# Second layer's attention: the queries' sums of squares in four units between products, and the key row behind the rotation of the queries

## The chip, the cores and the metric

The kernel runs on one core of one Trainium2 chip. The core has a matrix engine (TensorE, PE in the profile; PEld is its loading of weights), a vector engine (DVE), a scalar engine (ACT), GpSimd (POOL) and a queue that issues transfers (SP). Each engine works through its own list of instructions and waits on semaphores of the others. The metric is the device time of one execution in microseconds (us), the median of three runs; lower is better. For this kernel a difference of 0.3%, some 4.9 us, is about what a measurement can tell from none.

## The reference, cut to what matters

The program is two transformer blocks in float32 on 512 tokens of width 1024. The change lies in the second layer of the first block, an attention of eight heads:

```python
def mla_layer(x, positions, k_sh, v_sh, norm_g, w_in, q_lat_g, w_q_up, q_gain, w_out, mk, mv, mq_gain):
    ...
    q = (rmsnorm(q_lat, q_lat_g) @ w_q_up).reshape(bsz, s, B_HEADS, QK_HEAD)
    q = rmsnorm(q, q_gain)
    q = jnp.concatenate([q[..., :QK_NOPE], rope(q[..., QK_NOPE:], positions)], axis=-1)
    attn = chunk_causal_attention(q, k_sh, v_sh).reshape(bsz, s, B_WIDTH)
    y_b = attn * jax.nn.silu(z)
    ...
```

A query or key of a head has 192 numbers: 128 without a position and 64 that are rotated by the position. Both are normalised by the root of their mean square over all 192. The kernel does not scale queries and keys before the product: it multiplies the scores of a query by its factor, and the scores of a key by the key's. So it needs, for each head and token, the sum of squares of the query and of the key.

## The kernel before, in words

Every float32 product is made of three products of a coarse and a fine half (`mm3`, lines 519 to 522): high by high, high by low, low by high. So weights are split on the way: ACT writes the high half (`whi`, line 285 or 292), DVE the low one (`wlo`, line 286 or 293). Activations are split in the same way in `split` (lines 534 to 540).

The program is a list of units that is worked through in order; there is no scheduler behind it, and each engine's instructions stand in the order in which the units issue them. A unit that multiplies by weights leaves a second part (its post, for instance a split of the product) that is issued when the next unit begins; between units, pieces of the next weights' split are issued on ACT and DVE.

The eight heads go in four groups of two (g = 0 to 3). `prep(g)` makes what a group needs, as a list of units:

- `kn(h)`: the keys of one head (`kn`, and their squares); `kss(h)`: the keys' sums of squares by products with a column of ones (`ssk`). The second one starts the inverse root (`rsqrt`: two DVE instructions, then ten small POOL instructions that end in `rsx`, line 562).
- `qr`: the 64 rotated numbers of both heads' queries in one product, their squares, and the split for the rotation (`rph`, `rpl`); `qn(h)`: the other 128 of each head.
- `krow`: the key factors as rows. PE transposes them (`rkT`, line 1425), ACT copies them out (`rr`, 1427), POOL stores them to DRAM (`rd`, 1429) and then, when that has landed, loads them back broadcast over 128 partitions for each head (`rkb`, 1432).
- `qrot`: the rotation (`rope_rotate`): two products on PE (`rot`), three DVE instructions (`ra`, `rb`, `ra`; lines 1265 to 1267), then a split of the result: `qrh` on ACT, `qrl` on DVE.
- `qss`: the queries' sums of squares (`ssq`): for each of four blocks of 128 tokens one product with a two-column matrix and two with a column of ones, each of which the profile shows as two instructions, 24 in all; then the inverse root.
- `vu(0)`, `vu(1)`: the values.

`attend(g)` has eight scores, one for each head and block of queries. A score is: products on PE (`sc`), a DVE pass that multiplies by `rkb` and takes the maximum (line 1496), `nb`, the exponential on ACT, then on DVE the reciprocal and `e` times it (1505, 1506), then transposes of `e` on PE (`pt`, 1512), and their split into `PTh` and `PTl`. After four scores the product with the values follows (`po`). In the list, a score, the normalisation of the one before it and the transposes of the one two before it make a step; the units of the next group's `prep` and of the output product of the group before (`outproj`, `op`: six products of 512 columns to a unit) are dealt out between the eleven steps (`weave`).

The first group's `prep` has no attention beside it: it stands alone behind the gates' products.

Of the kernel before, what the change touches and what calls it, by code (L numbers as in the profile page):

```python
# [26 lines left out]
def block_kernel(ctx: ExitStack, tc: tile.TileContext, A: dict, out: bass.AP, stop=None):  # L27
# [23 lines left out]
    def bank(shape, name):  # L51
        return psum.tile(shape, F32, tag="b", name=name)

    def T(name="t", dt=F32):
        return tmp_p.tile([128, 512], dt, tag="T", name=name)

    def tiny(n, name):
        return tiny_p.tile([128, n], F32, tag=name, name=name)

    def pair(p, shape, tag, bufs=None):  # L60
        kw = {} if bufs is None else {"bufs": bufs}
        return (p.tile(shape, F32R, tag=tag + "h", name=tag + "h", **kw),
                p.tile(shape, F32R, tag=tag + "l", name=tag + "l", **kw))
# [244 lines left out]
    def U(fn, *keys, early=False, quiet=False):  # L308


        return (fn, keys, early, quiet)

    def add(*units):
        for u in units:
            if isinstance(u, list):
                add(*u)
            else:
                prog.append(u)
# [223 lines left out]
    def newton(v, n, eng=None, tiles=None):  # L542

        y, x, t = tiles or (tiny(n, f"{n_}{n}") for n_ in ("rsy", "rsx", "rst"))
        eng = eng or pool
        dve.tensor_scalar(out=y.bitcast(I32), in0=v.bitcast(I32), scalar1=-0.5, scalar2=float(0x5F19E900), op0=ALU.mult, op1=ALU.add)  # L546
        eng.tensor_tensor(out=x, in0=y, in1=y, op=ALU.mult)  # L547
        if n == 1:
            eng.tensor_scalar(out=x, in0=x, scalar1=v, scalar2=-0.7468889355659485, op0=ALU.mult, op1=ALU.add)
            src = x  # L550
            for c, by in ((-0.87124263, x), (0.77787455, x), (-0.77461322, x), (1.15710291, y)):
                eng.tensor_scalar(out=t, in0=src, scalar1=c, scalar2=by, op0=ALU.add, op1=ALU.mult)
                src = t
            return t
        eng.tensor_tensor(out=x, in0=x, in1=v, op=ALU.mult)

        for o, a in ((t, -0.33874717354774475), (x, -1.5906518697738647)):
            eng.tensor_scalar(out=o, in0=x, scalar1=a, scalar2=None, op0=ALU.add)
            eng.tensor_tensor(out=o, in0=o, in1=o, op=ALU.mult)
        for o, b, by in ((t, 0.8454821109771729, y), (x, 0.4313766062259674, t)):  # L560
            eng.tensor_scalar(out=o, in0=o, scalar1=b, scalar2=None, op0=ALU.add)
            eng.tensor_tensor(out=o, in0=o, in1=by, op=ALU.mult)
        return x

    def rsqrt(ssq, n, inv_d, post=1.0):
        v = tiny(n, "nv" if n == 1 else f"rsv{n}")
        dve.tensor_scalar(out=v, in0=ssq, scalar1=inv_d / post ** 2, scalar2=EPS / post ** 2, op0=ALU.mult, op1=ALU.add)
        return newton(v, n)
# [817 lines left out]
    H = {}  # L1386

    def prep(g):
# [11 lines left out]
        def kn(h):  # L1400
            def post(ps):
                sq = H["ksq", g, h] = T("sq")
                act.activation(out=sq, in_=ps, func=AF.Square)
                k = H["kn", g, h] = pair(bh.p, [128, 512], "kn", bufs=3)
                split(k[0], k[1], ps, scale=g_nope)

            return fmu(kkey, 128 * h, post, src="cT", nk=2)

        def kss(h):
            def fn():  # L1410
                if h == 0:
                    H["kss", g] = bank([128, 2, 4], "ssk")
                sq = H.pop(("ksq", g, h))
                for tb in range(4):
                    pe.matmul(out=H["kss", g][:, h, tb:tb + 1], lhsT=sq[:, tb * 128:tb * 128 + 128], rhs=ones, start=True, stop=True)
                if h == 1:
                    sk = tiny(8, "fac").rearrange("p (a b) -> p a b", a=2)
                    dve.tensor_tensor(out=sk, in0=H.pop(("kss", g)), in1=S["ssp"].unsqueeze(1).to_broadcast([128, 2, 4]), op=ALU.add)
                    H["rk", g] = rsqrt(sk.rearrange("p a b -> p (a b)"), 8, 1.0 / 192)

            return U(fn)
# [33 lines left out]
        def qn(h):  # L1455
            def post(ps):
                sq = T("sq")
                H["qsq", g].append(sq)
                act.activation(out=sq, in_=ps, func=AF.Square)
                q = H["qn", g, h] = pair(bh.p, [128, 512], "qn", bufs=3)  # L1460
                split(q[0], q[1], ps)

            return fmu(qkey, 128 * h, post, src="qlT", nk=3)

        def qss():
            sp = bank([128, 4, 2], "ssq")
            sqs = H.pop(("qsq", g))
            for tb in range(4):
                t = slice(tb * 128, tb * 128 + 128)
                pe.matmul(out=sp[:, tb, :], lhsT=sqs[0][:, t], rhs=blk1, start=True, stop=False)  # L1470
                for h in range(2):
                    pe.matmul(out=sp[:, tb, h:h + 1], lhsT=sqs[1 + h][:, t], rhs=ones, start=False, stop=h == 1)
            H["cq", g] = rsqrt(sp.rearrange("p a b -> p (a b)"), 8, 1.0 / 192, post=192 ** -0.5)

        qr = fmu(qkey, 256, qr_post, src="qlT", nk=3)
        return ([kn(0), kss(0), kn(1), kss(1), qr, qn(0), qn(1), U(krow), U(qrot), U(qss)],
                [vu(0), vu(1)])

    def attend(g):
# [56 lines left out]
    def pt_view(i, j):  # L1536
# [3 lines left out]
        return S["PT"][i][:, at:at + 384 * (j + 1)].rearrange("p (k c) -> p k c", c=384)[:, :, c:c + 128]  # L1540

    preps = [prep(g) for g in range(4)]
    add(U(open_bh))
    add([preps[0][0][i] for i in (0, 2, 1, 4, 3, 5, 6, 7, 8, 9)], preps[0][1])
    for g in range(4):
        m = outproj(f"oB{g - 1}", b_w_out, 2 * (g - 1), 2, slots=((g - 1) % 2,)) if g else []
        if g < 3:
            p = preps[g + 1][0]
            if g:
                m = m[0:2] + p[0:1] + m[2:4] + p[1:2] + m[4:6] + p[2:3] + m[6:8] + p[3:]  # L1550
            else:
                a0 = attend(0)
                add(weave(a0[0:6], p[0:1] + ob[4:5] + p[1:2] + ob[5:7] + p[2:3] + ob[7:8] + p[3:4]), weave(a0[6:], p[4:]), preps[1][1])
                continue
        if g < 3:
            add(weave(attend(g), m, lead=0), preps[g + 1][1])
        else:
            st3 = attend(g)
            ckl, ckn, _ = mem_norm(mem2_in, A["g_mem_2"], None, raw=lambda i: [S["bz"][:, 2 * i + h, :] for h in range(2)],
                                   gp=lambda: [S["bz"][:, 4 + h, :] for h in range(2)])  # L1560
            oB2 = m
            add(ckl, weave(st3[0:5], m[0:4]))
# [674 lines left out]
```

## Time and profile before

| | |
|---|---|
| median of 3 runs | 1630.41 us (1627.05 to 1632.39) |
| the profiled execution | 1630.76 us, its span 1629.0 us |
| PE busy | 1559.9 us (96%) |
| DVE, ACT, POOL busy | 1071.3, 743.3, 312.5 us |
| mean granted clock of PE | 0.987 |

The span is what the trace covers, so the execution has 1.8 us around it. A granted clock of 1.00 is 2.4 GHz, one of 0.50 is 1.2 GHz. The attention of the second layer lies between 645 and 842 us. A profile's row gives the start, the duration, the engine, the line, the instruction with its output and inputs, its shape, and in brackets how long the engine sat idle ahead of it and which instruction ended that. Rows of neighbours with one line are merged, and matmuls overlap, so that a start is a better mark than a duration.

### The profile page before, as it was taken

Reading aid. Unit: us, or ns where it says so; the run is one execution under the profiler, and the core shown is the slowest. Engines: PE = TensorE matmul, PEld = TensorE weight load, DVE = VectorE, ACT = ScalarE, POOL = GpSimd, SP = SyncE. Lnnn points to the kernel's source line nnn. Section 1 sums busy time; section 2 is a strip of 40 time slices with the busy share of each in tenths; the row PEclk is TensorE's granted clock in tenths of the full one; section 3 lists DMA queues with packets and bytes.
Section 4 is the critical chain, followed back from the end, with each engine's and each line's share of the span. In section 5 each row is a group of like instructions: output and inputs, shape, how many; then the busy total and the mean of one; then the engine's idle time right before and its main releaser. Section 6 shows DMA issues by size and latency. Waiting matters only on the chain. (4 is left out here: it accounts for less than half of the span.)

```text
span 1629.0 us, 24253 instructions
## 1 busy us (share of the span) xinstructions
PE 1559.9 (96%) x9385; PEld 1354.0 (83%) x9385; DVE 1071.3 (66%) x1980; ACT 743.3 (46%) x1538; POOL 312.5 (19%) x570
## 2 busy tenths in 40 slices
PE   6999999999999999999989999989999999999996
PEld 6889898988788888778869877868878889898986
DVE  6567646565685563667777555577456579686968
ACT  5344424333465544445544333455333463636353
POOL 4100000000030100211211000012100265555552
PEclk9999999999999999999999999999999999999998
DMA  8422223221332221212324331233312224141411
GB/s 265 140 78 70 87 78 90 67 92 65 129 112 83 91 78 35 92 35 67 124 72 148 116 118 52 73 109 117 99 70 73 76 85 156 52 156 52 142 53 52
DMA packets 134795, 152.75 MB, mean 94 GB/s; under 512 B 7616, under 2 KB 120024, under 8 KB 134680
## 3 DMA queue, kind: packets, MB, share of 16 engines
q1 hardware_dynamic: 131800, 143.58, 27.7%
q0 software_dynamic: 2304, 6.57, 1.4%
q8 instruction: 74, 1.21, 0.3%
q10 hardware_dynamic: 576, 1.05, 0.2%
q14 instruction: 41, 0.34, 0.1%
HBM read 144.88 MB, written 6.31 MB: 93 GB/s over the span
## 5 line engine op out<-in xcount | busy, mean ns | idle before, releaser
L520 PE MATMUL fm<-xth,whi 128*128 128x512 f32 (+1 forms) x824 | 307.3, 373 | 1.0 <-ACT whi L285 0.8
L521 PE MATMUL fm<-xtl,whi 128*128 128x512 f32 (+1 forms) x824 | 305.9, 371 | 1.5 <-DVE xtl L537 1.5
L522 PE MATMUL fm<-xth,wlo 128*128 128x512 f32 (+1 forms) x824 | 305.0, 370 | 0.1
L286 DVE TENSOR_TENSOR wlo<-wraw,whi 128x512 fp32r<-128x512 f32 (+2 forms) x324 | 206.3, 680 | 32.8 <-ACT whi L285 23.3
L285 ACT ACTIVATE whi<-wraw 128x512 fp32r<-128x512 f32 (+2 forms) x324 | 182.7, 619 | 38.8 <-PE op L522 23.3
L521 PEld LDWEIGHTS fm<-xtl,whi 128*128 128x128 f32 x824 | 156.0, 189 | 28.8 <-DVE xtl L537 2.5
L520 PEld LDWEIGHTS fm<-xth,whi 128*128 128x128 f32 x824 | 155.9, 189 | 28.4 <-ACT whi L285 1.0
L522 PEld LDWEIGHTS fm<-xth,wlo 128*128 128x128 f32 x824 | 155.7, 189 | 27.9 <-DVE wlo L286 0.5
L547 POOL TENSOR_TENSOR rsx<-rsy 128x1 f32<-128x1 f32 (+2 forms) x49 | 15.1, 307 | 753.8 <-DVE rsy L546 707.7
L520 PE MATMUL tm<-whi,xth 128*128 128x256 f32 x416 | 116.4, 280 | 0.0
L521 PE MATMUL tm<-wlo,xth 128*128 128x256 f32 x416 | 115.8, 278 | 0.0
L522 PE MATMUL tm<-whi,xtl 128*128 128x256 f32 x416 | 115.7, 278 | 0.0
L669 DVE TENSOR_TENSOR xall<-op,xall 128x512 f32<-128x512 f32 x120 | 81.7, 686 | 47.3 <-PE op L522 47.0
L522 PE MATMUL dn<-whi,ffgl 128*128 128x256 f32 x296 | 82.8, 280 | 0.0
L521 PE MATMUL dn<-wlo,ffgh 128*128 128x256 f32 x296 | 82.7, 279 | 0.0
L520 PE MATMUL dn<-whi,ffgh 128*128 128x256 f32 x296 | 82.6, 279 | 0.0
L521 PEld LDWEIGHTS tm<-wlo,xth 128*128 128x128 f32 x416 | 78.7, 189 | 0.2
L520 PEld LDWEIGHTS tm<-whi,xth 128*128 128x128 f32 x416 | 78.7, 189 | 0.2
L522 PEld LDWEIGHTS tm<-whi,xtl 128*128 128x128 f32 x416 | 78.7, 189 | 0.0
L520 PE MATMUL op<-whi,y0h 128*128 128x512 f32 x160 | 66.8, 417 | 0.0
L522 PE MATMUL op<-whi,y0l 128*128 128x512 f32 x160 | 64.0, 400 | 0.0
L521 PE MATMUL op<-wlo,y0h 128*128 128x512 f32 x160 | 63.8, 399 | 0.0
(590 smaller groups left out, 4038.5 us busy)
## 6 DMA issues: line engine op xcount, KB each, us to landing
wraw<-in_a_w_in_dram SPq DMA_DIRECT2D x23, 1024.0 KB
wraw<-in_w_down_dram SPq DMA_DIRECT2D x19, 512.0 KB
wraw<-in_mem_w_kv_dram SPq DMA_DIRECT2D x8, 1024.0 KB
wraw<-in_b_w_in_dram SPq DMA_DIRECT2D x8, 1024.0 KB
wraw<-in_w_ckv_dram SPq DMA_DIRECT2D x8, 1024.0 KB
wraw<-in_w_in_dram SPq DMA_DIRECT2D x8, 1024.0 KB
wx<-in_w_down_dram SPq DMA_DIRECT2D x13, 512.0 KB
wraw<-in_a_w_out_dram SPq DMA_DIRECT2D x6, 1024.0 KB
```

The source lines that it names most:

```text
L285: act.activation(out=hi[:, s], in_=t[:, s], func=AF.Copy)
L286: dve.tensor_tensor(out=lo[:, s], in0=t[:, s], in1=f(hi)[:, s], op=ALU.subtract)
L520: pe.matmul(out=ps, lhsT=lh, rhs=rh, start=first, stop=False)
L521: pe.matmul(out=ps, lhsT=lh, rhs=rl, start=False, stop=False)
L522: pe.matmul(out=ps, lhsT=ll, rhs=rh, start=False, stop=last)
L547: eng.tensor_tensor(out=x, in0=y, in1=y, op=ALU.mult)
L669: return lambda: dve.tensor_tensor(out=xs[tb][h], in0=ps, in1=xs[tb][h], op=ALU.add)
```

## The change

Three things. `qss` becomes four units, one for each block of tokens, and the inverse root is issued by the last. In the list of `prep` the rotation (`qrot`) now stands ahead of the key row (`krow`), and the four units behind both. And the lists are dealt out anew: ahead of the first group two of the four units go between its two value products; in groups 1 and 2 the `prep` of the next group comes earlier and the last two of the eight units of the output product stand between the small units.

```diff
-        def qss():
-            sp = bank([128, 4, 2], "ssq")
-            sqs = H.pop(("qsq", g))
-            for tb in range(4):
+        def qss(tb):
+            def fn():
+                if tb == 0:
+                    H["qsp", g] = bank([128, 4, 2], "ssq")
+                sp, sqs = H["qsp", g], H["qsq", g]
                 t = slice(tb * 128, tb * 128 + 128)
                 pe.matmul(out=sp[:, tb, :], lhsT=sqs[0][:, t], rhs=blk1, start=True, stop=False)
                 for h in range(2):
                     pe.matmul(out=sp[:, tb, h:h + 1], lhsT=sqs[1 + h][:, t], rhs=ones, start=False, stop=h == 1)
-            H["cq", g] = rsqrt(sp.rearrange("p a b -> p (a b)"), 8, 1.0 / 192, post=192 ** -0.5)
+                if tb == 3:
+                    H.pop(("qsq", g))
+                    H["cq", g] = rsqrt(H.pop(("qsp", g)).rearrange("p a b -> p (a b)"), 8, 1.0 / 192, post=192 ** -0.5)
+
+            return U(fn)
 
         qr = fmu(qkey, 256, qr_post, src="qlT", nk=3)
-        return ([kn(0), kss(0), kn(1), kss(1), qr, qn(0), qn(1), U(krow), U(qrot), U(qss)],
+        return ([kn(0), kss(0), kn(1), kss(1), qr, qn(0), qn(1), U(qrot), U(krow)] + [qss(tb) for tb in range(4)],
                 [vu(0), vu(1)])
...
-    add([preps[0][0][i] for i in (0, 2, 1, 4, 3, 5, 6, 7, 8, 9)], preps[0][1])
+    add([preps[0][0][i] for i in (0, 2, 1, 4, 3, 5, 6, 7, 8, 9, 10)], preps[0][1][0:1], preps[0][0][11:13], preps[0][1][1:2])
...
-                m = m[0:2] + p[0:1] + m[2:4] + p[1:2] + m[4:6] + p[2:3] + m[6:8] + p[3:]
+                m = m[0:2] + p[0:1] + m[2:4] + p[1:2] + m[4:6] + p[2:10] + m[6:7] + p[10:12] + m[7:8] + p[12:]
```

What this does to the engines' lists shows at three places. The first is ACT ahead of the first group; `rr` is the copy of the key row, `qrh` the high half of the rotated queries. Before:

```order
L536 ACTIVATE qnh<-fm 128x512
L292 ACTIVATE whi<-wraw,cols 128x256 x2
L1427 COPY rr<-rkT 8x128
L536 ACTIVATE qrh<-ra 128x512
L536 ACTIVATE Vh<-V 128x512 x2
```

and now:

```order
L536 ACTIVATE qnh<-fm 128x512
L292 ACTIVATE whi<-wraw,cols 128x256 x2
L536 ACTIVATE qrh<-ra 128x512
L1427 COPY rr<-rkT 8x128
L536 ACTIVATE Vh<-V 128x512 x2
```

The copy of the key row has moved behind the high half of the rotation, which waits for DVE.

The second is DVE at the end of group 0, from the last score's `nb` on. Before:

```order
L1498 SCALAR_TENSOR_TENSOR nb<-mx,rsx_6579 128x1
L537 TENSOR_TENSOR qnl<-fm,qnh 128x512
L537 TENSOR_TENSOR PTl<-pt,PTh 128x2x128
L1505 RECIPROCAL rc<-sm 128x1
L1506 TENSOR_SCALAR e<-e,rc 128x512
L537 TENSOR_TENSOR qnl<-fm,qnh 128x512
L286 TENSOR_TENSOR wlo<-wraw,whi 128x512 x2
L537 TENSOR_TENSOR PTl<-pt,PTh 128x3x128
L286 TENSOR_TENSOR wlo<-wraw,whi 128x512 x2
L537 TENSOR_TENSOR PTl<-pt,PTh 128x4x128
L1265 SCALAR_TENSOR_TENSOR ra<-fm,cols,cosT 128x512
```

and now:

```order
L1503 SCALAR_TENSOR_TENSOR nb<-mx,rsx_6596 128x1
L537 TENSOR_TENSOR qnl<-fm,qnh 128x512 x2
L286 TENSOR_TENSOR wlo<-wraw,whi 128x512 x2
L537 TENSOR_TENSOR PTl<-pt,PTh 128x2x128
L1510 RECIPROCAL rc<-sm 128x1
L1511 TENSOR_SCALAR e<-e,rc 128x512
L286 TENSOR_TENSOR wlo<-wraw,whi 128x512 x2
L1265 SCALAR_TENSOR_TENSOR ra<-fm,cols,cosT 128x512
L1266 TENSOR_TENSOR rb<-rot,sinT 128x512
L1267 TENSOR_TENSOR ra<-ra,rb 128x512
L537 TENSOR_TENSOR qrl<-ra,qrh 128x512
L537 TENSOR_TENSOR PTl<-pt,PTh 128x3x128
```

The normalised `e` of the last score has moved behind a second `qnl` and two splits of weights, and the last two splits of `PT` (of three and of four tiles) behind the four instructions of the rotation; they stood ahead of it.

The third is DVE at the end of group 1 (group 2 has the same). Before:

```order
L1498 SCALAR_TENSOR_TENSOR nb<-mx,rsx_7073 128x1
L1418 TENSOR_TENSOR fac<-ssk,ssp 128x8
L567 TENSOR_SCALAR rsv_7450<-fac 128x8
L546 TENSOR_SCALAR rsy_7452<-rsv_7450 128x8
L540 SCALAR_TENSOR_TENSOR rpl<-fm,cols,rph 128x512
L537 TENSOR_TENSOR PTl<-pt,PTh 128x2x128
L1505 RECIPROCAL rc<-sm 128x1
L1506 TENSOR_SCALAR e<-e,rc 128x512
```

and now:

```order
L1503 SCALAR_TENSOR_TENSOR nb<-mx,rsx_7073 128x1
L1265 SCALAR_TENSOR_TENSOR ra<-fm,cols,cosT 128x512
L1266 TENSOR_TENSOR rb<-rot,sinT 128x512
L1267 TENSOR_TENSOR ra<-ra,rb 128x512
L537 TENSOR_TENSOR qrl<-ra,qrh 128x512
L537 TENSOR_TENSOR PTl<-pt,PTh 128x2x128
L1510 RECIPROCAL rc<-sm 128x1
L1511 TENSOR_SCALAR e<-e,rc 128x512
```

Between `nb` and `e` of the last score now stand the four instructions of the rotation.

## Rows read from the trace of the kernel before

**Rows 1.** The page's first part: busy us, share of the span, instructions.
```profile
PE 1559.9 (96%) x9385; PEld 1354.0 (83%) x9385; DVE 1071.3 (66%) x1980; ACT 743.3 (46%) x1538; POOL 312.5 (19%) x570
```

**Rows 2.** Ends of groups 0 to 2, stretches of 10 us: busy times, granted clock.
```profile
core 0: us, PE busy (x) PEld busy (x) DVE busy (x) ACT busy (x) POOL busy (x), PEclk, DMA share, GB/s
702.00:712.00 10.00, 10.00 (x66) 9.44 (x67) 8.54 (x16) 4.34 (x9) 3.53 (x10) 0.83 0.39 112
750.00:760.00 10.00, 9.56 (x63) 8.94 (x63) 8.41 (x15) 4.91 (x11) 3.59 (x11) 0.83 0.48 111
798.00:808.00 10.00, 9.63 (x62) 8.95 (x62) 8.34 (x16) 4.91 (x11) 4.15 (x12) 0.83 0.54 153
```

**Rows 3.** PE in order of time, end of group 0: start us, us, instruction.
```profile
695.30 0.23 PE L1493 MATMUL sc<-masks,idb 128*128 128x128 bf16 x1
...
701.97 0.63 PE L1512 MATMUL pt<-ident,e 128*128 128x128 f32 x4 [1.53 <-DVE e L1506]
...
705.95 0.79 PE L521 MATMUL po<-PTl,Vh 128*128 128x512 f32 x1
```

**Rows 4.** PE in order of time, group 1.
```profile
740.90 0.23 PE L1493 MATMUL sc<-masks,idb 128*128 128x128 bf16 x1
...
753.27 0.57 PE L521 MATMUL po<-PTl,Vh 128*128 128x512 f32 x1 [0.44 <-DVE PTl L537]
```

**Rows 5.** PE in order of time, ahead of and in the first steps of group 0.
```profile
656.45 0.48 PE L1259 MATMUL rot<-rph,prm 128*128 128x512 f32 x1
...
657.00 0.28 PE L1470 MATMUL ssq<-blk,sq 128*128 128x2 f32 x2
...
659.60 0.37 PE L520 MATMUL V<-whi,cTh 128*128 128x256 f32 x1
...
666.05 0.48 PE L520 MATMUL op<-whi,y0h 128*128 128x512 f32 x1
...
667.54 0.50 PE L520 MATMUL op<-whi,y1h 128*128 128x512 f32 x1
668.27 0.51 PE L521 MATMUL op<-wlo,y1h 128*128 128x512 f32 x1 [0.23 <-DVE wlo L286]
```

**Rows 6.** ACT in order of time, ahead of group 0.
```profile
657.94 0.24 ACT L1427 COPY rr<-rkT 8x128 f32<-8x128 f32 x1
660.79 0.64 ACT L536 ACTIVATE qrh<-ra 128x512 fp32r<-128x512 f32 x1 [2.61 <-DVE ra L1267]
```

**Rows 7.** POOL in order of time, ahead of group 0: loads, first and last of an inverse root.
```profile
660.38 1.14 POOL L1432 DMA_DIRECT2D rkb<-rd  x2 [1.32 <-DMA rd<-rr]
662.52 0.20 POOL L547 TENSOR_TENSOR rsx<-rsy 128x8 f32<-128x8 f32 x1 [0.99 <-DVE rsy L546]
...
665.88 0.20 POOL L562 TENSOR_TENSOR rsx<-rsx,rst 128x8 f32<-128x8 f32 x1
```

**Rows 8.** Transfers issued from 660 to 666 us: KB each, us to landing.
```profile
rkb<-rd POOLq DMA_DIRECT2D x2, 256.0 KB, 4.3
```

**Rows 9.** DVE in order of time, first score of group 0.
```profile
665.15 0.28 DVE L1496 CUSTOM_DVE_ANT_0 e<-sc,rkb 128x128 f32<-128x128 f32 x1
...
666.12 0.16 DVE L1498 SCALAR_TENSOR_TENSOR nb<-mx,rsx 128x1 f32<-128x1 f32 x1 [0.69 <-POOL rsx L562]
```

**Rows 10.** DVE in order of time, end of group 0.
```profile
698.05 0.16 DVE L1498 SCALAR_TENSOR_TENSOR nb<-mx,rsx 128x1 f32<-128x1 f32 x1
...
701.34 0.49 DVE L1506 TENSOR_SCALAR e<-e,rc 128x512 f32<-128x512 f32 x1
...
702.34 1.28 DVE L286 TENSOR_TENSOR wlo<-wraw,whi 128x512 fp32r<-128x512 f32 x2
...
705.21 0.68 DVE L537 TENSOR_TENSOR PTl<-pt,PTh 128x512 fp32r<-128x512 f32 x1
705.81 0.74 DVE L1265 SCALAR_TENSOR_TENSOR ra<-fm,cols,cosT 128x512 f32<-128x512 f32 x1
...
708.58 0.69 DVE L537 TENSOR_TENSOR qrl<-ra,qrh 128x512 fp32r<-128x512 f32 x1 [0.70 <-ACT qrh L536]
```

**Rows 11.** DVE in order of time, last score of group 1.
```profile
743.68 0.16 DVE L1498 SCALAR_TENSOR_TENSOR nb<-mx,rsx 128x1 f32<-128x1 f32 x1
```

## The prediction

> **What bounds the kernel now.** I read the page's busy table first: PE is busy 96% of the span [rows 1], so what delays PE lengthens the execution, and what the others do counts only where PE waits for it. Then I went through PE's timeline over the four groups, for idle gaps and for products that start further apart than their neighbours of the same shape. Three places lose time, all at a group's end. In group 0 the transposes of the last score wait 1.53 us for its normalised `e` [rows 3]; in group 1 the product with the values waits 0.44 us for the split of those transposes [rows 4]; group 2 looks like group 1. And behind each of the three runs of 24 small `ssq` instructions the granted clock falls to 1.2 GHz: over the 10 us around each it is 0.83 on average [rows 2], that is 10 x 0.17 = 1.7 us lost, three times, 5.1 us in all. Nothing on PE is more than that to be won here. Last I read, on ACT, DVE and POOL, what stands ahead of the instructions that PE waits for, since the change moves just those.
>
> **The change part by part.** The arithmetic is the same: 24 `ssq` instructions to a group, which take 2.6 us in one run (657.00 to 659.60, [rows 5]), now four units of 0.65. No instruction is added, so the terms are the waits that the new order makes and unmakes.
>
> *Key row behind the rotation, ahead of group 0.* ACT copied the key row at 657.94 and only then waited 2.61 us for DVE's rotation to write `qrh` at 660.79 [rows 6]. Now the copy stands behind `qrh`. The rotation's DVE work does not move, so `qrh` stays at 660.79, the copy comes at about 661.35, 3.4 us later, and everything hung on it too: POOL's two loads of `rkb` go from 660.38 to about 663.8 [rows 7], and with 4.3 us to landing [rows 8] the first is there at 668.1, where DVE used it at 665.15 [rows 9]. Queued behind the loads on POOL is the inverse root of the queries: it ran from 662.52 to 666.08 and can now not begin before 663.8 + 1.14 = 664.95 [rows 7], 2.4 us later. DVE's `nb` already waited 0.69 us for that root, at 666.12 [rows 9], so it moves to about 668.5. Behind `nb` stand the exponential on ACT and then the third piece of the output weights' split, for which PE already waited at 668.27 [rows 5]; that product moves to about 670.7. Delay of PE: 2.4 us, from 1.6 (if the root runs 0.8 us faster with DVE idle beside it) to 3.4 (all of the copy's delay). I take 2.2. What PE gains ahead of it, 0.3 us by no longer waiting for the key factors with the rotation unissued, goes into the same wait and counts nothing.
>
> *End of group 0.* Before, DVE normalised the last `e` at 701.34 and PE took it 0.63 us later [rows 3, 10]. Now a second `qnl` (0.6 us) and two splits of weights (1.2 of the 1.28 us row, which overlaps its neighbour) stand ahead of it, and the second `qnl` waits some 0.4 us for ACT (an estimate): `e` at about 703.5, transposes at 704.2. Behind `e` come two more weight splits (1.2), then the rotation, from the start of `ra` to the start of `qrl` 2.77 us (705.81 to 708.58, of which 0.70 is a wait for ACT [rows 10]), `qrl` 0.6, the split of three tiles 0.5 and that of four, on which `po` depends: its start is 703.9 + 1.2 + 2.77 + 0.6 + 0.5 = 709.0. PE's second `po` product followed that start by 0.74 us before (705.21 to 705.95 [rows 3, 10]), so it comes at 709.8 instead of 705.95: 3.85 us later. All of PE's own work up to there, two `ssq` units behind the transposes, is done by 706 and hides nothing more. The 1.7 us of low clock that followed before will very likely follow again, as PE now idles twice within 8 us; if it does not, the loss is 2.15, if it lasts twice as long, 5.55. I take 3.85.
>
> *Ends of groups 1 and 2.* In both groups before, `nb` of the last score began 2.8 us behind the last product of its scores (695.30 to 698.05, 740.90 to 743.68 [rows 3, 4, 10, 11]); what stands ahead of it now (two `qnl`, two splits of weights, in place of two additions to `xall` and the same splits) is as long. Between `nb` and `e` now stands the rotation: 0.1 + 2.77 + 0.6 for `qrl` + 0.3 for a split of two tiles + 0.2 for the reciprocal = 4.0, and PE takes `e` 0.63 after its start: transposes 7.4 us behind the scores. PE's own work in that time: rotation 0.55 (656.45 to 657.00), key transpose and five `pt` some 0.6, three `ssq` units 2.0, one `op` unit 1.5 (666.05 to 667.54 [rows 5]), together 4.65. So PE waits up to 2.8 us where it did not wait before; I take 2.4, since `nb` may come a little earlier with DVE less crowded, and 1.6 as the least. The last `op` unit and `ssq` unit (2.1 us) then cover the split for `po`, whose 0.44 us of wait goes. The clock: the stretch between the two `op` units, 0.3 + 1.3 + 2.4 + 0.4 = 4.4 us, has no wide product, against 2.6 us of `ssq` that brought the clock down before. I put the low clock at half its old price, 0.9, from 0 to 1.7. New loss 2.4 + 0.9 = 3.3, old loss 0.44 + 1.7 = 2.1: each group 1.2 us slower, from -0.5 to +2.4.
>
> The stretch has one weighing to add. Transposes on PE ran between the products in every such place here, at a granted clock of 0.83 over the 10 us [rows 2], and the trace cannot say whether they held it up. The Trainium skill, TensorE: Matmul & The Clock Gate, Part 4 on transposes, says that transposes do not count as activity of the engine in the way that products do. By that rule the new stretch is as good as idle and the clock falls in both groups at the full 1.7, which makes the sum 1.6 us longer than mine; if they count like products, it falls in neither, and the sum is 1.8 us shorter.
>
> *What costs nothing.* The earlier `prep` units of groups 1 and 2 want the weights for the queries sooner; their split now has some 2.3 us of PE work over it (two transposes, a score, a `kss`), about as long as it takes, so I count 0, at most 0.3 a group. The key row of groups 1 to 3 is needed only by the next group's first score, behind `po` and eight value products; its delay of 4 to 5 us in group 0 stays under these.
>
> Sum: 2.2 + 3.85 + 2 x 1.2 = 8.45 us on the profiled execution's 1630.76, which is 1639.2; that execution lies 0.35 above the median shown, so 1638.8 against the median of 1630.41. I say 1639. The ends of the terms give 2.75 and 13.75 us: 1633.2 to 1644.2.
>
> **The rivals.**
> - *The spread does what it is for (faster).* The small products stand between wide ones, the clock stays at 2.4 GHz at all three ends, and the waits are no longer than before: 5.1 us less, 1625.3. For it: the three stretches of low clock follow the three unbroken runs, and nothing else in the groups brings the clock down [rows 2]. Against it: the last `e` would have to be there 4.65 us behind its scores in groups 1 and 2, and DVE's list puts 4.0 us behind an `nb` that itself comes after 2.8. It decides from a wait of under 0.5 us at these transposes on. The Trainium skill, TensorE: Matmul & The Clock Gate, in the table under "Why this matters for your kernels", advises to avoid idle gaps between bursts; by that advice alone this rival would hold, but the gaps here are made by DVE's order, not by the small products. Chance 0.06.
> - *Waits for low clock, one for one (no change).* PE waits as I say, but at full clock behind each wait, and the root ahead of group 0 runs fast: the low ends of the terms, 2.75 us, or a little less if DVE catches up: 1632.5. For it: a low clock costs nothing while PE waits anyway, and after a wait all of PE's work up to the next group is wide. Against it: the new gaps with what lies around them are longer than the 2.6 us of `ssq` that each brought the clock down. Chance 0.17.
> - *The clock stays down after every wait (much slower).* Four waits of over 2 us, each followed by twice the low clock: the upper ends and more, 1645. For it: in group 0 PE idles twice in a row. Against it: the 1.7 us lost at each fall before, at half speed, mean that each lasted some 3.4 us, no longer [rows 2]. Chance 0.05.
> - My forecast, 1639: chance 0.72.
>
> **How the numbers follow.** Of the forecast's 0.72, some 0.05 lies within 0.3% (4.9 us, about what a measurement of this kernel can tell from no change), by the low ends of its terms; the rest is slower. The no-change rival adds 0.17, and of the faster one's 0.06 a sixth lies within the bound. That gives faster 0.05, same 0.23, slower 0.72. The range of 8 in 10 goes from 1631.5, which takes in most of the no-change case, to 1645, just above the upper ends of the terms.
>
> **What would show it.** In the profile of the changed kernel: ACT's `rr` right behind `qrh` ahead of group 0, the first `nb` some 2.4 us later, and a PE wait of 2 to 3 us for `wlo` in the second `op` unit of that group. At the end of group 0 two waits of PE, about 2 us for `e` and 3 to 4 us for `PTh` or `PTl`. In groups 1 and 2 a wait of 2 to 3 us for `e` at the four transposes and none at `po`. The granted clock falls behind group 0's waits; in groups 1 and 2 it may. I am wrong if PE's waits in the four places sum to under 4 us, or if the three dips are gone and the time falls under 1627.

## The result and the profile after

The changed kernel takes 1645.54 us (median of 5 runs, 1640.31 to 1648.65) against 1630.41 (5 runs, 1627.05 to 1632.39). The ratio is 1.0093, with an interval of 1.0067 to 1.0119: slower by 15.1 us. The profiled execution took 1647.57 us with a span of 1645.8, 16.8 us more than the span of before.

The page's first part for the changed kernel, to be read against [rows 1]:

```profile
PE 1565.3 (95%) x9385; PEld 1358.0 (83%) x9385; DVE 1071.0 (65%) x1980; ACT 742.9 (45%) x1538; POOL 310.3 (19%) x570
```

The number of instructions is the same. PE is busy 5.4 us longer with the same products, and its share fell all the same: some products ran slower and some of its time was spent waiting.

Where the time went is seen from one instruction that each group has in the same place: the mask product that closes a score. First the changed kernel (PE in order of time: the first score of groups 0 to 3, and behind that of group 0 its fourth), then the kernel before:

```profile
662.39 0.23 PE L1498 MATMUL sc<-masks,idb 128*128 128x128 bf16 x1
...
682.70 0.23 PE L1498 MATMUL sc<-masks,idb 128*128 128x128 bf16 x1
...
722.77 0.23 PE L1498 MATMUL sc<-masks,idb 128*128 128x128 bf16 x1
...
774.06 0.23 PE L1498 MATMUL sc<-masks,idb 128*128 128x128 bf16 x1
...
825.39 0.23 PE L1498 MATMUL sc<-masks,idb 128*128 128x128 bf16 x1
```

```profile
663.49 0.23 PE L1493 MATMUL sc<-masks,idb 128*128 128x128 bf16 x1
...
676.79 0.23 PE L1493 MATMUL sc<-masks,idb 128*128 128x128 bf16 x1
...
713.06 0.23 PE L1493 MATMUL sc<-masks,idb 128*128 128x128 bf16 x1
...
760.42 0.23 PE L1493 MATMUL sc<-masks,idb 128*128 128x128 bf16 x1
...
807.74 0.23 PE L1493 MATMUL sc<-masks,idb 128*128 128x128 bf16 x1
```

The differences (now less before) are -1.10, +5.91, +9.71, +13.64 and +17.65 us. So the first four scores of group 0 (the "head" below) cost 7.0 us, the rest of group 0 3.8, group 1 3.9 and group 2 4.0. What follows gives back 0.85.

PE at these places in the changed kernel (against [rows 3 to 5]; the number in brackets is the wait, and who ended it):

```profile
668.84 0.50 PE L520 MATMUL op<-whi,y1h 128*128 128x512 f32 x1 [2.24 <-ACT whi L285]
669.56 0.51 PE L521 MATMUL op<-wlo,y1h 128*128 128x512 f32 x1 [0.23 <-DVE wlo L286]
...
676.20 0.63 PE L522 MATMUL op<-whi,y0l 128*128 128x512 f32 x1
676.62 0.63 PE L520 MATMUL op<-whi,y0h 128*128 128x512 f32 x1
...
701.21 0.23 PE L1498 MATMUL sc<-masks,idb 128*128 128x128 bf16 x1
...
710.08 0.66 PE L1517 MATMUL pt<-ident,e 128*128 128x128 f32 x4 [2.00 <-DVE e L1511]
...
714.92 0.79 PE L520 MATMUL po<-PTh,Vh 128*128 128x512 f32 x1 [2.96 <-ACT PTh L536]
715.71 0.79 PE L521 MATMUL po<-PTl,Vh 128*128 128x512 f32 x1
...
762.66 0.63 PE L1517 MATMUL pt<-ident,e 128*128 128x128 f32 x4 [2.30 <-DVE e L1511]
...
813.96 0.63 PE L1517 MATMUL pt<-ident,e 128*128 128x128 f32 x4 [2.30 <-DVE e L1511]
```

The waits are those that were forecast: 2.24 us for the third piece of the output weights (ended by ACT's `whi`, with 0.23 us more for the `wlo` that the forecast named), 2.00 for `e` and 2.96 for `PTh` at the end of group 0, 2.30 for `e` in groups 1 and 2. What had not been forecast is seen in the starts of the `op` products at 676.20 and 676.62: 0.42 us apart, where such products start 0.23 us apart at the full clock (in the kernel before at 809.45 and 809.68 us, in group 3). The windows of the changed kernel around the four places, and a piece of the second (the column behind POOL is the granted clock):

```profile
core 0: us, PE busy (x) PEld busy (x) DVE busy (x) ACT busy (x) POOL busy (x), PEclk, DMA share, GB/s
669.00:682.00 13.00, 12.74 (x38) 9.25 (x39) 5.73 (x18) 3.13 (x8) 0.00 (x0) 0.61 0.07 20
711.00:721.00 10.00, 7.04 (x39) 6.26 (x39) 5.31 (x11) 2.69 (x6) 3.81 (x13) 0.66 0.40 112
712.30:714.90 2.60, 0.00 (x0) 0.00 (x0) 1.87 (x4) 1.63 (x4) 0.57 (x1) 0.50 0.86 216
761.00:771.00 10.00, 8.34 (x35) 7.54 (x36) 6.58 (x14) 2.92 (x7) 3.99 (x13) 0.66 0.16 53
812.50:822.50 10.00, 8.54 (x37) 7.70 (x38) 6.52 (x14) 2.75 (x7) 4.10 (x13) 0.66 0.19 54
```

A clock of 0.61 over 13 us means 13 x 0.39 x 2 = 10 us at 1.2 GHz, and 0.66 over 10 us means 6.8 us. Before, the three ends had 3.4 us each [rows 2], and the head none (1.00 from 666 to 676 us). At these four places that is 31 us at the low clock in place of 10. PE loses half of what it works in: up to 10 of the 16.8 us are the clock's, less what ran while PE waited (2.6 us from 712.30, clock 0.50, PE busy 0.00).

The engines that PE waited for, in the changed kernel: ACT, POOL and DVE in order of time, one fence each (against [rows 6, 7, 9 to 11]).

```profile
660.10 0.63 ACT L536 ACTIVATE qrh<-ra 128x512 fp32r<-128x512 f32 x1 [2.74 <-DVE ra L1267]
660.64 0.24 ACT L1427 COPY rr<-rkT 8x128 f32<-8x128 f32 x1
```

```profile
661.17 0.58 POOL L1429 DMA_DIRECT2D rd<-rr  x1 [5.48 <-ACT rr L1427]
663.09 1.14 POOL L1432 DMA_DIRECT2D rkb<-rd  x2 [1.33 <-DMA rd<-rr]
```

```profile
667.01 0.29 DVE L1501 CUSTOM_DVE_ANT_0 e<-sc,rkb 128x128 f32<-128x128 f32 x1 [2.85 <-DMA rkb<-rd]
...
667.42 0.16 DVE L1503 SCALAR_TENSOR_TENSOR nb<-mx,rsx 128x1 f32<-128x1 f32 x1
...
709.53 0.48 DVE L1511 TENSOR_SCALAR e<-e,rc 128x512 f32<-128x512 f32 x1
...
711.14 0.74 DVE L1265 SCALAR_TENSOR_TENSOR ra<-fm,cols,cosT 128x512 f32<-128x512 f32 x1
...
713.90 0.69 DVE L537 TENSOR_TENSOR qrl<-ra,qrh 128x512 fp32r<-128x512 f32 x1 [0.69 <-ACT qrh L536]
714.51 1.15 DVE L537 TENSOR_TENSOR PTl<-pt,PTh 128x384 fp32r<-128x384 f32 x2
...
758.05 0.16 DVE L1503 SCALAR_TENSOR_TENSOR nb<-mx,rsx 128x1 f32<-128x1 f32 x1
758.13 0.74 DVE L1265 SCALAR_TENSOR_TENSOR ra<-fm,cols,cosT 128x512 f32<-128x512 f32 x1
...
762.02 0.49 DVE L1511 TENSOR_SCALAR e<-e,rc 128x512 f32<-128x512 f32 x1
```

The key row's copy stands behind `qrh`, the two loads of `rkb` follow, and DVE waits 2.85 us for them; `nb` comes 5.03 us behind the first score where it came 2.63 behind it. At the end of group 0 the rotation (`ra`, `qrl`) stands between `e` and the splits, in group 1 between `nb` and `e`.

### The profile page after: what moved, and what is told of

Its sections match the earlier page's. It is cut to its first block, busy times and chain, and to the rows that moved or that the text cites. A ratio compares the mean times of both kernels' runs of the same rounds, so it can differ in the third digit from the quotient of the medians.

```text
span 1645.8 us, 24249 instructions
## 1 busy us (share of the span) xinstructions
PE 1565.3 (95%) x9385; PEld 1358.0 (83%) x9385; DVE 1071.0 (65%) x1980; ACT 742.9 (45%) x1538; POOL 310.3 (19%) x570
## 4 chain that ended last, share of the span: by engine, by line
PE 72%; DVE 12%; ACT 5%; issue 4%; POOL 3%; DMA 2%; SPq 0%; DVEq 0%; ACTq 0%; POOLq 0%
PE fm L520 10%; PE fm L522 10%; PE fm L521 10%; PE op L521 3%; PE op L520 3%; PE op L522 3%; PE dn L522 3%; PE dn L521 3%; PE dn L520 3%; PE tm L520 3%; PE tm L521 3%; PE tm L522 3%; DVE wlo L286 2%; PE sc L520 1%; DVE wlo L293 1%
```

## The experiments

Each ran beside the kernel before. "Theory 1" is that PE's waits behind the moved rotation, and the low clock behind the waits, make the loss. The rival is that the spread of the small products does.

| kernel | median us | ratio to before, interval |
|---|---|---|
| e1_head | 1640.63 | 1.0067 (1.0053 to 1.0082) |
| e2_swap | 1648.80 | 1.0113 (1.0097 to 1.0130) |
| e3_last | 1633.20 | 1.0019 (1.0010 to 1.0028) |
| e4_norot | 1639.20 | 1.0063 (1.0049 to 1.0077) |
| e5_op | 1636.10 | 1.0036 (1.0024 to 1.0048) |
| e6_wide | 1627.23 | 0.9985 (0.9976 to 0.9993) |
| e7_wait | 1640.37 | 1.0064 (1.0052 to 1.0076) |
| e8_g0 | 1642.15 | 1.0072 (1.0060 to 1.0084) |
| e9_between | 1631.99 | 1.0008 (0.9999 to 1.0017) |
| e10_again | 1643.31 | one run |
| e11_tails | 1639.50 | 1.0054 (1.0038 to 1.0070) |
| e12_headswap | 1634.76 | 1.0024 (1.0011 to 1.0036) |

### Which part of the change costs what

**e1_head**, the changed kernel with the old order ahead of group 0 (7 is the rotation, 8 the key row):

```diff
-(0, 2, 1, 4, 3, 5, 6, 7, 8, 9, 10)
+(0, 2, 1, 4, 3, 5, 6, 8, 7, 9, 10)
```

> The changed kernel with one difference: in the list of units ahead of group 0 the key row stands in front of the rotation again; groups 1 to 3 stay as changed. Theory 1 (the loss is made of PE's waits behind the moved rotation and of the low clock that follows each wait): the wait of 2.24 us for the third piece of the output weights and the low clock behind it (10.2 us at half speed, 4.85 us of delay) go, and the time falls by about 7 us, to 1638.5 (1636 to 1641). Theory 2 (the loss comes from the small products and their new places between the wide ones, not from the place of the rotation): the small products here stay spread, so the time stays at 1645 (1643 to 1647).

PE's wait at the head is 0.42 us, the clock stays up, and the head costs 0.55 us by its masks. The median falls by 4.9 us, to theory 1's side, but by less than the 7 expected: 7 was the head of one profiled execution, and e4, e8 and e12 below show heads of 2.2 to 5.5 us with the same order.

**e12_headswap**, the same edit the other way round, on the kernel before:

```diff
-(0, 2, 1, 4, 3, 5, 6, 7, 8, 9)
+(0, 2, 1, 4, 3, 5, 6, 8, 7, 9)
```

> The kernel before with the rotation put in front of the key row ahead of group 0 alone. Theory 1 (wait for the key row's trip through DRAM and then low clock): PE waits 2.1 to 4.1 us for the third piece of the output weights, low clock behind it, 1635 (1633.5 to 1637.5). Forecast as on record, a wait with no clock behind it: 1632.4. Rival (the head costs only together with the spread between the value products): 1630.

4.6 us slower, as theory 1 had it; the order ahead of group 0 alone is enough. In its profile PE waits longer than in the changed kernel, and POOL shows why (the write of the key row to DRAM, then its two loads; the bracket is the wait for that write):

```profile
662.62 0.59 POOL L1429 DMA_DIRECT2D rd<-rr  x1 [5.48 <-ACT rr L1427]
666.75 1.14 POOL L1432 DMA_DIRECT2D rkb<-rd  x2 [3.54 <-DMA rd<-rr]
```

The 4 KB write `rd` was waited for 3.54 us, against 1.33 in the changed kernel.

Behind the head its lists are those of the kernel before, and still the clock does not repeat what it did there: at the end of group 0, with the old wait (1.53 us), it is low for 6.8 us in place of 3.4, and at the end of group 2, with the old wait (0.37 us) and the run of 24 narrow products from 804.38 to 806.97 us, it does not fall at all:

```profile
802.00:816.00 14.00, 13.63 (x94) 11.99 (x93) 11.24 (x21) 8.51 (x18) 4.88 (x14) 1.00 0.40 115
```

**e2_swap**, the kernel before with only the two units exchanged in all four lists:

```diff
-U(krow), U(qrot), U(qss)]
+U(qrot), U(krow), U(qss)]
```

> The kernel before with one difference: rotation in front of the key row in all four lists; the sums of squares stay one run of 24 and all products keep their places. Theory 1: the head loses its 7 us as in the changed kernel (a wait of 2 to 3 us for the output weights, then low clock), and at the ends of groups 0 to 2 the rotation now stands one step earlier, ahead of the last split of the transposes, so PE waits 1 to 3 us there for that split: 1640 to 1648. Theory 2 (only the spread costs): 1630.4 as before (1628 to 1632).

1648.8, 0.8 us above the top of theory 1's range, and the rival's 1630.4 is out. With no spread at all the exchange costs more than the whole change: PE waits 4.10 us at the head, and 2.50, 3.23 and 3.23 us for the last `PTh` at the ends of groups 0 to 2, since the rotation now stands ahead of that split.

**e8_g0**, the changed kernel with the units at the end of group 0 dealt as before:

```diff
-weave(a0[6:], p[4:])
+*[weave(a0[6 + i:7 + i], u) for i, u in enumerate((p[4:5], p[5:6], p[6:7], p[8:9], p[7:8] + p[9:]))]
```

> The changed kernel with the units at the end of group 0 dealt to its steps as before (first qn, second qn, key row, rotation, each a step later; the four units of sums of squares one behind the other at the end); the head and groups 1 and 2 stay as changed. Theory 1: the two waits there (2.00 for e, 2.96 for the split) become one of 1.5, and the low clock behind them shrinks from 6.8 to 3.4 us: 3.8 us less, 1641.7 (1639.5 to 1643.5). Theory 2 (the end of group 0 costs nothing, the head and the later groups cost it all): 1645.

3.4 us less than the changed kernel, as expected; the two waits became one of 1.51.

**e11_tails**, both edits (e1 and e8) at once, so that only groups 1 and 2 stay as changed:

> The changed kernel with the head's order (key row in front of the rotation) and the dealing at the end of group 0 as before; only the spread and the new dealing of groups 1 and 2, and the spread units at the head and of group 0's last step, stay. If the three places add up (head 4.9 and end of group 0 3.4 us by the two kernels that undid one each), what stays is 15.5 less 8.3 us, 7 us for the ends of groups 1 and 2: 1637.3 (1636 to 1639). If their waits cost only what was forecast, 1.2 us each: 1632.5. If low clock at one place sets off what follows at the next, so that the places do not add up: under 1632 or over 1640.

1639.5, 9.3 us over before and 2 more than expected, just outside the range given. The interval (6.2 to 11.4 us over before) holds the expected 7; the forecast's 2.4 us for both groups is out. In its profile 8.8 us arise in groups 1 and 2 (low clock of 10.2 and 6.8 us behind waits of 2.33 and 2.31), and 1.4 at the end of group 0, where the one wait of 1.54 was followed by 6.8 us at the low clock.

**e3_last**, the changed kernel with the spread kept and the rotation put last:

```diff
-U(qrot), U(krow)] + [qss(tb) for tb in range(4)],
+U(krow)] + [qss(tb) for tb in range(4)] + [U(qrot)],
```

(and ahead of group 0 key row, rotation, units.)

> The changed kernel with the spread kept and the rotation put behind the fourth unit of sums of squares in groups 1 to 3; ahead of group 0 the order is key row, rotation, units, with the units still spread between the value products. Theory 1: the waits behind the rotation go (2.24 at the head, 2.96 for the split at the end of group 0, 2.30 at each of groups 1 and 2) and most of the low clock behind them; the wait of 2.0 us for the last e of group 0, behind two splits of queries and two of weights, stays with its low clock: 1628 to 1634. Theory 2: the spread is kept, so the time stays above 1640. If the small products were the only cause of the three old stretches of low clock, spread ones leave none: 1625.

1633.2: 12.3 us of the 15.1 are gone with the spread still there, so the rival falls. The windows around the ends of groups 0 to 2 and the start of group 3:

```profile
702.00:712.00 10.00, 8.57 (x53) 7.66 (x54) 8.50 (x18) 4.67 (x11) 4.88 (x13) 0.83 0.40 112
750.00:760.00 10.00, 9.61 (x69) 8.79 (x69) 8.47 (x17) 3.79 (x10) 4.62 (x13) 1.00 0.16 53
797.00:807.00 10.00, 9.61 (x69) 8.79 (x68) 8.51 (x17) 3.76 (x9) 4.99 (x14) 1.00 0.26 80
812.00:820.00 8.00, 6.38 (x24) 4.14 (x22) 5.79 (x21) 2.76 (x8) 0.00 (x0) 0.79 1.00 339
```

At the ends of groups 1 and 2 the clock stays at 1.00 in this profile: the spread does what the rival of the forecast expected of it, where PE hardly waits (0.39 us for `e`). It is not faster than before: DVE begins the last rotation 1.6 us later (802.63 us, 801.05 before) and has two more splits of output weights behind it, and PE waits at a place where it had not waited, for the first `e` of group 3:

```profile
814.04 0.30 PE L1517 MATMUL pt<-ident,e 128*128 128x128 f32 x1 [1.62 <-DVE e L1511]
```

**e5_op**, e3_last with the last two `op` units dealt earlier in groups 1 and 2, to take that wait away:

```diff
-p[2:10] + m[6:7] + p[10:12] + m[7:8] + p[12:]
+p[2:6] + m[6:7] + p[6:9] + m[7:8] + p[9:]
```

> The kernel of e3_last with the last two units of the output product dealt earlier in groups 1 and 2 (one before the second qn, one behind the first unit of sums of squares), so that DVE's work for them is done before the end of the group. If the 1.62 us for which PE waited for the first e of group 3 in e3_last came from that work, it goes with the 3.4 us of low clock behind it (3.3 us together); against it PE has 0.9 us less of its own work in front of the product with the values, so that product waits about 1 us at the ends of groups 1 and 2. Theory 1 (what costs is PE's waits and the low clock behind them): 1631 (1628 to 1634), faster than the kernel before only if no low clock follows the two waits of 1 us. Theory 2 (the spread itself costs): 1633 or more.

Missed, at 1636.1: by its time alone this is on the rival's side (1633 or more). The profile shows another reason than the spread: the wait in group 3 is gone, but PE waits 1.46 and 1.47 us, not 1, for `PTl` at the ends of groups 1 and 2, with 3.4 and 6.8 us of low clock behind them.

### What brings the clock down

**e4_norot**, the changed kernel without DVE's three rotation operations in groups 1 to 3 (the queries stay unrotated):

```diff
-rope_rotate(H.pop(("qrs", g)), S["cos"], S["sin"], q)
+st = H.pop(("qrs", g))
+if g == 0:
+    rope_rotate(st, S["cos"], S["sin"], q)
+else:
...
+    pe.matmul(out=pr, lhsT=prm, rhs=h, start=True, stop=False)
+    pe.matmul(out=pr, lhsT=prm, rhs=l, start=False, stop=True)
+    split(q[0], q[1], ps, scale=gain)
```

> The changed kernel, every unit in its place, but in groups 1 to 3 DVE leaves out the three operations of the rotation (PE's two products stay; the queries go on unrotated), so some 2.2 us of DVE work in front of e and of the splits goes. Theory 1 (the waits bring the clock down): the head stays (7 us), the wait of 2.96 at the end of group 0 falls to about 0.8, those of groups 1 and 2 from 2.3 to about 0.1, and the low stretches of 6.8 us at the ends of groups 1 and 2 shrink to 3.4 or less: 1645.5 less 2.2, less twice 2.2, less 2 to 5 for the clock, is 1634 to 1637. Theory 2 (the low clock comes of the small products and transposes alone, wait or no wait): the low stretches stay at 6.8 us and only part of the 6.6 us of waits is won: 1639 to 1642.

Not decided: the median, 1639.2, lies in the rival's range, at its lower edge, and the profiled execution (1633.93, the fastest of six) just below theory 1's. The waits in groups 1 and 2 were 1.22 and 1.49 us, more than the 0.1 expected. In the profiled execution there is no low clock at either of those ends, with the same small products and transposes. That would speak for theory 1, but e8 and e10 each have one such end without low clock behind the full wait of 2.3 us, so two ends of one execution do not settle it; of the slower executions there is no profile.

**e7_wait** is the cleaner test: e3_last, every product in its place, with 2 us of idle DVE work in front of the last `e` of groups 1 and 2:

```diff
+if g in (1, 2) and h == 1 and j == 3:
+    jk = T("rb")
+    for i in range(3):
+        dve.tensor_tensor(out=jk, in0=S["cos"], in1=S["sin"], op=ALU.mult)
```

> The kernel of e3_last, every product in its place, with three idle DVE products of 128x512 (2.0 us) in front of the last e of groups 1 and 2. In e3_last PE waits 0.39 us there and the clock stays up. PE should wait 2.4 us now in both. Theory 1 (the wait brings the clock down): low stretches of 3.4 to 6.8 us appear at both ends: 1633.2 plus 4.0 for the waits plus 3.4 to 6.8 for the clock, 1640 to 1644. Theory 2 (the clock goes by the products, and these are unchanged): no low clock there, 1637 (1636 to 1638).

1640.37, which is theory 1's. PE waits 2.45 and 2.44 us, and the clock that had been 1.00 at both ends in e3_last falls (windows of e7_wait around the same two ends):

```profile
754.00:764.00 10.00, 7.55 (x39) 6.66 (x39) 8.21 (x16) 1.75 (x3) 3.43 (x13) 0.83 0.20 53
805.00:815.00 10.00, 7.81 (x41) 6.93 (x42) 8.19 (x16) 2.71 (x5) 4.03 (x13) 0.83 0.25 80
```

From the first score of group 1 to that of group 2 it takes 3.6 us longer than e3_last: about the 2.06 of added wait and half of the 3.4 us at the low clock.

**e6_wide**, the kernel before, where 18 of the 24 small products are replaced by 9 wide ones in groups 1 to 3 (one block of sums is used for all four):

```diff
...
+for i in range(9):
+    pe.matmul(out=bk, lhsT=q0[:, 0:128], rhs=q0, start=True, stop=True)
...
-for tb in range(4):
+for tb in range(4) if g == 0 else (3,):
```

> The kernel before, but in groups 1 to 3 only one of the four blocks of sums of squares is computed and used for all four, and the 18 small products left out (2.0 us) are replaced by 9 products of 128x512 whose results nobody reads (2.1 us): PE's time and its waits stay, the narrow products go. Theory A (only PE's waits bring the clock down): the waits of 1.53, 0.44 and 0.37 us stay, so the three stretches of low clock at the ends of groups 0, 1 and 2 stay, 1630 (1628 to 1632). Theory B (the run of narrow products brings it down, as do waits): the low stretches at the ends of groups 1 and 2 vanish, the one of group 0 perhaps; 3.4 to 5.1 us less: 1626 (1624 to 1627.5).

2.8 us faster, theory B's side. The three windows of [rows 2] in this kernel:

```profile
702.00:712.00 10.00, 8.97 (x60) 8.19 (x60) 8.50 (x18) 4.93 (x11) 2.63 (x8) 1.00 0.37 110
750.00:760.00 10.00, 9.63 (x63) 8.42 (x62) 8.54 (x16) 5.32 (x12) 3.88 (x13) 1.00 0.45 112
797.00:807.00 10.00, 9.70 (x66) 8.41 (x65) 8.54 (x16) 5.03 (x10) 4.99 (x14) 1.00 0.53 159
```

All three dips are gone in this profile, that of group 0 too, though PE still waits 1.55 us for `e` there. So the waits of before need not bring the clock down by themselves, and the run of narrow products has a part in its fall. How large a part is less sure: e12 has one such end without a dip, with all 24 products in place. What holds beyond the one profile is the median, 2.8 us less over 11 runs (interval 1.1 to 3.9). By the masks its three groups take 4.5 us less than before; part of that goes again in group 3, where PE waits 1.15 us for an `e` and 3.4 us of low clock follow. So 2.8 us is about what keeping the clock up there can win.

**e9_between**, the kernel before with the rotation's two wide products put between the blocks of sums, and nothing else moved:

```diff
+qss(0)
 pe.matmul(out=pr, lhsT=prm, rhs=h, start=True, stop=False)
+qss(1)
 pe.matmul(out=pr, lhsT=prm, rhs=l, start=False, stop=True)
...
+qss(2)
+qss(3)
```

> The kernel before with one difference, on PE alone: in all four groups the first block of sums of squares (6 products) stands in front of the rotation's first product, the second block between its two products, the other two behind; nothing is moved on DVE, ACT or POOL, and PE has as much work in front of the product with the values as before. Theory 1 (an unbroken run of narrow products brought the clock down at the ends of groups 0 to 2 before, and an added wait does so too): if two wide products are enough to break the run, the three low stretches go, 1626 (1624.5 to 1628); Theory 2: what counts is the whole stretch with next to no wide work, and two wide products do not change it: low stretches stay, 1630 (1628.5 to 1631.5). In both, no wait is added.

1632.0, not told apart from before: theory 2's side, half a microsecond above its range. In its profile the dip of group 1 is gone, that of group 2 is as before, and that of group 0 is longer (0.61 over the 13 us from 702).

**e10_again**, the changed kernel once more:

> The changed kernel itself, profiled once more. Theory 1 (how long the low clock lasts behind one and the same wait differs from execution to execution): the waits of 2.00, 2.96, 2.30 and 2.30 us are there again within 0.1, but the low stretches behind them have other lengths than 10.2, 6.8, 6.8 and 6.8 us, in at least two of the four places. Theory 2 (the length follows from the kernel): the same four lengths again, within one step of 3.4 us in one place.

The waits are 2.12, 2.01, 2.59, 2.30 and 2.31 us, nearly those of the first profile (the third is 0.37 shorter, outside the 0.1). The windows at the head and the ends of groups 0 to 2:

```profile
669.00:682.00 13.00, 12.74 (x38) 9.29 (x38) 5.43 (x18) 3.09 (x8) 0.00 (x0) 0.61 0.07 20
711.00:721.00 10.00, 7.41 (x42) 6.63 (x42) 5.62 (x12) 2.86 (x6) 3.80 (x13) 0.66 0.40 112
761.00:771.00 10.00, 8.78 (x51) 8.09 (x52) 7.40 (x16) 4.13 (x8) 4.02 (x11) 0.83 0.17 53
811.00:821.00 10.00, 8.98 (x63) 8.21 (x63) 8.72 (x18) 5.38 (x11) 5.31 (x15) 1.00 0.20 59
```

At the head and in group 0 the low clock lasts as long as in the first profile, in group 1 it lasts 3.4 in place of 6.8 us, and in group 2 there is none. One kernel, the same waits, other lengths.

With all the profiles the price of one wait can be laid beside the low clock that it met. The low clock is from the granted clock of the profile, as worked out above; the cost is how much the delay against the kernel before grows, by the masks, over the stretch:

| place, wait | low clock, us | cost, us (kernel) |
|---|---|---|
| ends of groups 1, 2: 2.30 to 2.33 | 0 | 0.9 (e8, e10) |
| | 3.4 | 2.4 (e1, e10) |
| | 6.8 | 3.9, 4.0 (changed), 4.0 (e8), 4.0 (e11) |
| | 10.2 | 4.9 (e1), 4.8 (e11) |
| head: 2.08 | 0 | 2.2 (e4) |
| head: 2.12, 2.24 | 10.2 | 6.8 (e10), 7.0 (changed) |
| head: 4.07 to 4.10 | 3.4 | 5.4 (e2), 5.5 (e8), 5.5 (e12) |

## Why the prediction was right and wrong

The direction held, and so did the waits: PE waits where it was said to wait, and nearly for as long. What the low clock behind a wait costs was wrong: +15.1 us against 8.6, half a microsecond above the upper end of the range. Two of the three terms were too small by it: the head, and the ends of groups 1 and 2.

- **Key row behind the rotation: the wait right, the term too small.** The copy came behind `qrh`, `nb` 2.40 us later (2.4 forecast), and PE waited 2.24 us. In detail it was the load of `rkb` and not the inverse root that DVE waited for. The step that failed is the last, "I take 2.2": it priced the wait alone and had no low clock behind it. The head costs 2.2 where none follows (e4) and 5.4 to 7.0 in the five other profiles with this order; the mean of the six is 5.4. In the changed kernel's two profiles the excess is the clock's (10.2 us low behind waits of 2.24 and 2.12); in e2, e8 and e12 the wait itself was 4.1 us, as the write of the key row took longer, and 3.4 us of low clock followed.
- **End of group 0: right in size, with the clock's part wrong.** The second product with the values came 3.85 us later, counted from the last score (715.71 - 701.21, against 705.95 - 695.30 in [rows 3]), which is the forecast's term. The cost was 3.8 us in the profiled execution, 3.5 in e10, and 3.4 by e8. The low clock there lasted 6.8 us, twice the old one, but began some 3 us ahead of that product, while PE waited (the window from 712.30); only the rest met work, some 4 us, about as much as the 3.4 before. The forecast would have priced a low stretch of twice the length at 5.55 us; that it came out at 3.85 all the same was in part luck.
- **Ends of groups 1 and 2: the wait right, the clock too cheap.** `nb` to `e` took 3.97 us (4.0 forecast), PE's own work covered the rest, and the wait was 2.30 (2.4 forecast); no wait was left at the product with the values. The step that failed is "I put the low clock at half its old price, 0.9". The stretch ranges from nothing to 10.2 us at 1.2 GHz, which is up to 5.1 us where PE works through it; over the ten ends in the table the mean cost is 3.2 us each, against 1.2.
- Taken together, from the means over several kernels: 5.4 + 3.6 + 2 x 3.2 = 15.4 us, against 15.1 measured.
- **The rival "the clock stays down after every wait"** came closest (1645), with a chance of 0.05. The argument against it, that each fall before had lasted 3.4 us and no longer, and the readings that three places lose time and that nothing but the small products brings the clock down in these groups, overlooked a fourth fall in the same trace. At the end of group 3, which has no such products, PE waited 2.54 us in the kernel before, and the clock stood at 1.2 GHz for 6.8 us (10 x 0.34 x 2):

```profile
836.19 1.11 PE L1512 MATMUL pt<-ident,e 128*128 128x128 f32 x4 [2.54 <-DVE e L1506]
```

```profile
833.00:843.00 10.00, 7.12 (x25) 5.51 (x25) 8.53 (x17) 3.30 (x7) 2.75 (x9) 0.66 0.18 54
```

  The change does not touch this end: the wait for that `e` is 2.52 to 2.54 us in all fourteen profiles, and the low clock there lasts 6.8 us in five of them and 3.4 in nine.
- **The rival "the spread does what it is for"** holds for the products and fails for the change, for the reason given against it: e3 keeps the clock up at two ends with the spread, and in e6 wide products in place of narrow ones are worth 2.8 us, of the 5.1 that the old dips cost.
- **The advice cited in the forecast.** The Trainium skill, TensorE: Matmul & The Clock Gate, table under "Why this matters for your kernels", advises to leave no idle gaps between bursts of products. In direction e7 agrees with it: with every product in its place, waits of 2.45 and 2.44 us in place of 0.39 went with a granted clock of 0.83 over 10 us in place of 1.00.
- **The transposes.** The forecast let its sum hang on whether transposes hold the clock up (1.6 us more, 1.8 us less). On the sentence that it took from the Trainium skill, TensorE: Matmul & The Clock Gate, Part 4, this case decides nothing: e6 keeps all transposes and its clock stays at 1.00 at three ends, but wide products stand around them.

What stays open: what sets the length of a low stretch behind a given wait, and why the write of the key row sometimes takes longer. No version here beats the kernel before and computes the same.

## What to carry to other kernels

Before spreading or exchanging units in a program whose order is written out, follow every instruction that moves with them on the slower engines: here the rotation's DVE work in front of `e` and one DRAM round trip cost some five times the 2.8 us that e6 lets one expect of the spread. Price a new wait of TensorE as the wait plus a low-clock stretch of uncertain length behind it, and take that length from several profiles, not from one. Before calling a length typical, look through the whole trace for other falls, also where the change does nothing: the trace before already held one of 6.8 us.

## What was not expected of the hardware

- Behind one and the same wait of 2.3 us the clock stayed up or stood at 1.2 GHz for 3.4, 6.8 or 10.2 us over the ten ends in the table, while PE was busy with wide products at half their rate. Two executions of the changed kernel alone differ at two of four places (6.8 and 3.4, 6.8 and none). The spread between executions is wider too, 1640.3 to 1648.7 us for the changed kernel and 1627.1 to 1632.4 for the one before; that the low clock makes it so is not shown.
- A run of 24 narrow products, 2.6 us in which PE counts as busy, went with a fall of the clock at three ends of the kernel before; with 9 wide ones in place of 18 of them there was none at the same three ends. The run does not bring the clock down every time: at the end of group 2 in e12 it stayed at 1.00.
- The same 4 KB write to DRAM landed after 1.6 us in three of the six profiles with the rotation first, and after 3.8 to 3.9 us in the other three; in all eight with the key row first it took 1.6.
